# The hand-over from the delta rule to the branch products: loads by token block, a last group kept on chip, the conv cache as side work, and the order of split products

## The chip, the cores and the metric

The kernel runs on one core of a Trainium2 chip. The metric is the time of one execution in microseconds on the device. The engines are PE (TensorE, matrix products, with a queue of weight loads PEld), DVE (VectorE), ACT (ScalarE), POOL (GpSimd) and SP (SyncE, which here only issues DMAs).

## The reference

One layer of a hybrid decoder for 1024 prompt tokens and 8 x 4 sample tokens, in float32:

```python
z = _rmsnorm(x, g_attn) @ w_in           # split into q, k, v, gates, ...
qkv, new_conv = _causal_conv(concat([qa, ka, va]), conv_buf, w_conv_a)
o_a, s_delta_new = _gated_delta(q, k, v, beta, g, s_delta)     # 4 heads, chunks of 64
o_a = _head_rmsnorm(o_a, g_out_a) * silu(oga);  y_a = o_a @ w_branch_a
o_b, s_hgrn_new = _hgrn2(qh, 1.0 - f, ib, log(f), s_hgrn)      # 4 heads, chunks of 32
o_b = _head_rmsnorm(o_b, g_out_b) * silu(ogb);  y_b = o_b @ w_branch_b
mix = sigmoid(gate_a) * y_a + sigmoid(gate_b) * y_b
x = x + mix @ w_out
x = x + (silu(conv(h2 @ w_ffn_gate)) * (h2 @ w_ffn_up)) @ w_ffn_down,  h2 = _rmsnorm(x, g_ffn)
```

Outputs are the final normed tokens, the last 3 rows ahead of the qkv convolution (`new_conv`), the states of both mixers, and the last rows of the FFN convolution. Model width is 1024, a head has 128 columns.

## The kernel before

Tokens lie along the free axis: T = 1024 + 32 = 1056 columns, in three blocks (NB) of BW = 352. A float32 operand of a large product is split in a high and a low half (`split`, L85 to L87: ACT casts the high half, L86, and DVE subtracts it for the low one, L87). A product of two split operands is three matmuls (`mm3`, L110 to L116): L114 high x high, L115 high weights x low data, L116 low weights x high data. `load_w` loads a weight tile `wraw` and splits it into `whi` and `wlo`, in pools of two buffers.

The span runs through these stages: norm and first projections (0 to 57 us), groups of the HGRN2 mixer (180 to 430), four groups of the gated delta rule (`gdn_group`, 256 tokens each, 430 to 783), the branch products (800 to 890), the product with `w_out`, and the FFN with its down product (1000 to 1760).

The projections that the groups don't need at once form a queue, `fill`. Each generator of a group yields numbers as it goes, and `drive` hands each to `fill`, which emits as many projection steps; a step is 24 matmuls 128x352. So the groups' chains of small work (DVE, ACT, DMA round trips) are woven with `fill` products on PE. Every second yield, `drive` also takes one step of the first generator in `side`. A scheduler then fixes the order of each engine.

In a `gdn_group`, L731 and L732 make `UA`; DMAs take its diagonal blocks to DRAM and back as `Db`; DVE inverts them in 15 steps (L765, L767); DMAs carry the result `X` over DRAM to `Yd`; after a `yield 2.4`, DVE transposes it (`Xd`, L780) and PE goes on at L786, L794, L807 and further small products to L869. `head_post` norms the group's output `o_sb` (L596), transposes it on PE (L603) and gates it (L605) into `og`, which L887 stores to `oT_d[0]`. `og` was loaded at L885 from `og_d`; its tile has the tag "z" of pool `mz`, two buffers.

After the four groups `store_conv_cache` transposes 12 tiles of `cout` on PE (L250), copies them on ACT (L252) to `rowt`, also tag "z", and stores that (L253, L254). Then the pool `post` opens. Three loads bring both mixers' outputs from `oT_d` into `raw` (L1184), with fill steps between; the rest of the queue drains; ACT and DVE split `raw` into `ohi` and `olo`, in blocks of 352 columns (the first block head by head, the others two heads at a time). `ohi` and `olo` take the buffers of `hhi` and `hlo`, which the fill products read. The last fill products make the gates, `sg` (L570, ACT), stored to `sg_d` (L571). The branch products follow: for each pair of output tiles and block, gates `sga` and `sgb` are loaded (L1208), four outputs are made in the four banks of `psd` (tile `pd`), DVE multiplies each with its gate (L1215), adds (L1216) and the sum is split to `mhi` and `mlo`. SP issues loads in order, and every engine's instructions run in the order of the scheduler.

## Time and profile before

| | us |
|---|---|
| median of 3 runs | 1765.17 (1764.98, 1765.17, 1772.67) |
| profiled execution | 1772.35 |
| its span | 1770.6 |
| PE busy in the span | 1723.2 |

The rows below come from the profiled execution. A timeline row is start, duration, engine, line, operation, tiles as out<-in, shape and count; brackets at its end give the idle time ahead of it and what ended it. Durations of PE are modelled and overlap: products of 128x352 that are 0.32 us long start 0.16 us apart.

### The profile page before, as it was taken

What the parts mean: (1) busy time and instruction counts of PE and PEld (TensorE: products, weight loads), DVE (VectorE), ACT (ScalarE), POOL (GpSimd) and SP (SyncE); (2) the same over time, 40 slices, a digit from 0 to 9 for tenths busy, and PEclk for the clock granted to TensorE, in tenths of its full rate; (3) what the DMA queues carried; (4) which work ended last, traced back from release to release, by engine and by line L of the source; (5) the groups of instructions that cost most, each with busy time, mean ns of one, the idle gap of its engine ahead of it and who ended that gap; (6) DMA issues with size and microseconds to landing.
All of it is one profiled execution on the core that took longest, in us unless ns stands there. A gap on an engine that the chain in (4) does not pass through costs nothing.

```text
span 1770.6 us, 31215 instructions
## 1 busy us (share of the span) xinstructions
PE 1723.2 (97%) x13345; PEld 1629.3 (92%) x13345; DVE 839.5 (47%) x1448; ACT 535.2 (30%) x1249; POOL 138.0 (8%) x226
## 2 busy tenths in 40 slices
PE   7999999999999999989999999999999999999998
PEld 7999899989989998889999999989989989899887
DVE  5411546785545444426642634443453453444446
ACT  5443324443343434123110522212212112122134
POOL 2200001120102110100000100000000000000001
PEclk9999999999999999899999999999999999999999
DMA  6333334445253532245433111120110210210203
GB/s 205 108 96 107 108 110 152 141 121 158 78 162 93 170 110 86 57 161 178 122 98 90 54 49 35 38 72 25 48 48 24 72 48 24 72 48 24 72 28 112
DMA packets 200647, 159.52 MB, mean 90 GB/s; under 512 B 18638, under 2 KB 185184, under 8 KB 200489
## 3 DMA queue, kind: packets, MB, share of 16 engines
q1 hardware_dynamic: 171286, 119.14, 22.9%
q10 hardware_dynamic: 29222, 38.39, 6.3%
q8 instruction: 105, 1.72, 0.4%
q14 instruction: 34, 0.28, 0.0%
HBM read 117.74 MB, written 39.69 MB: 89 GB/s over the span
## 4 chain that ended last, share of the span: by engine, by line
PE 84%; DVE 6%; DMA 5%; issue 2%; ACT 2%; POOL 1%; SPq 1%; ACTq 0%; DVEq 0%; POOLq 0%
PE pd L114 20%; PE pd L116 20%; PE pd L115 20%; PE pd L1342 5%; PE pd L1344 4%; PE pd L1343 4%; DMA oT_d<-og 1%; DVE co L236 1%; DVE Pt L765 1%; DVE X L767 1%; PE pm L1010 1%; PE pm L1333 1%; DMA qf<-qf_d 1%; DMA Sb<-in_state_delta 1%; PE pm L191 0%
## 5 line engine op out<-in xcount | busy, mean ns | idle before, releaser
L114 PE MATMUL pd<-hhi,whi 128*128 128x352 f32 x1056 | 351.1, 332 | 0.0
L116 PE MATMUL pd<-hhi,wlo 128*128 128x352 f32 x1056 | 347.3, 329 | 0.0
L115 PE MATMUL pd<-hlo,whi 128*128 128x352 f32 x1056 | 346.7, 328 | 0.0
L114 PE MATMUL pd<-mhi,whi 128*128 128x352 f32 x1056 | 341.3, 323 | 0.0
L115 PE MATMUL pd<-mlo,whi 128*128 128x352 f32 x1056 | 339.1, 321 | 0.0
L116 PE MATMUL pd<-mhi,wlo 128*128 128x352 f32 x1056 | 339.0, 321 | 0.0
L87 DVE TENSOR_TENSOR wlo<-wraw,whi 128x1024 fp32r<-128x1024 f32 x126 | 153.5, 1227 | 203.3 <-ACT whi L86 201.6
L86 ACT CAST whi<-wraw 128x1024 fp32r<-128x1024 f32 x126 | 130.6, 1051 | 336.6 <-PE pd L1344 135.6
L114 PEld LDWEIGHTS pd<-hhi,whi 128*128 128x128 f32 x1056 | 201.5, 191 | 2.5 <-issue 1.4
L115 PEld LDWEIGHTS pd<-hlo,whi 128*128 128x128 f32 x1056 | 201.8, 191 | 1.2 <-issue 0.2
L116 PEld LDWEIGHTS pd<-hhi,wlo 128*128 128x128 f32 x1056 | 201.5, 191 | 1.0
L115 PEld LDWEIGHTS pd<-mlo,whi 128*128 128x128 f32 x1056 | 198.9, 188 | 0.4
L114 PEld LDWEIGHTS pd<-mhi,whi 128*128 128x128 f32 x1056 | 198.7, 188 | 0.4
L116 PEld LDWEIGHTS pd<-mhi,wlo 128*128 128x128 f32 x1056 | 198.5, 188 | 0.0
L1342 PE MATMUL pd<-whi,act 128*128 128x512 f32 x352 | 138.1, 392 | 0.0
L1343 PE MATMUL pd<-wlo,act 128*128 128x512 f32 x352 | 137.2, 390 | 0.0
L1344 PE MATMUL pd<-whi,act 128*128 128x512 f32 x352 | 137.2, 390 | 0.0
L1354 DVE TENSOR_TENSOR x<-x,pd 128x512 f32<-128x512 f32 x144 | 97.8, 686 | 78.8 <-PE pd L1344 78.8
L86 ACT CAST act<-ga 128x352 fp32r<-128x352 f32 (+1 forms) x66 | 31.5, 477 | 180.6 <-DVE ga L1314 180.5
L1342 PEld LDWEIGHTS pd<-whi,act 128*128 128x128 f32 x352 | 66.1, 188 | 21.0 <-DVE ga L1314 7.5
L1314 DVE TENSOR_TENSOR ga<-pd,ga 128x352 f32<-128x352 f32 x66 | 34.5, 522 | 100.8 <-PE pd L116 100.8
L223 ACT COPY z<-pd 128x352 f32<-128x352 f32 (+1 forms) x102 | 44.2, 441 | 124.7 <-PE pd L116 124.6
(417 smaller groups left out, 2568.3 us busy)
## 6 DMA issues: line engine op xcount, KB each, us to landing
wraw<-in_w_in SPq DMA_DIRECT2D x48, 512.0 KB
wraw<-in_w_ffn_gate SPq DMA_DIRECT2D x22, 512.0 KB
wraw<-in_w_ffn_up SPq DMA_DIRECT2D x22, 512.0 KB
wraw<-in_w_ffn_down SPq DMA_DIRECT2D x22, 512.0 KB
sg_d<-sg ACTq DMA_DIRECT2D x16, 528.0 KB
qkv_d<-sl ACTq DMA_DIRECT2D x12, 512.0 KB
sga<-sg_d SPq DMA_DIRECT2D x12, 352.0 KB
sgb<-sg_d SPq DMA_DIRECT2D x12, 352.0 KB
```

The source lines that it names most:

```text
L86: nc.scalar.copy(out=hi, in_=src)
L87: (eng or nc.vector).tensor_tensor(lo, src, hi.bitcast(F32), ALU.subtract)
L114: nc.tensor.matmul(ps, whi[:, kw], xhi[:, kx], start=q == 0, stop=False)
L115: nc.tensor.matmul(ps, whi[:, kw], xlo[:, kx], start=False, stop=False)
L116: nc.tensor.matmul(ps, wlo[:, kw], xhi[:, kx], start=False, stop=q == n - 1)
L223: nc.scalar.copy(out=z[:, pad + a:pad + e], in_=ps[:, :e - a])
L236: nc.vector.scalar_tensor_tensor(co, z[:, q:q + cw], wT[:, q:q + 1], co, ALU.mult, ALU.add)
L1314: nc.vector.tensor_tensor(a[:, bs], ps, a[:, bs], ALU.mult)
L1342: nc.tensor.matmul(ps, ahi[:, s0 + k, ts], W[0][:, k, qs], start=a, stop=False)
L1343: nc.tensor.matmul(ps, ahi[:, s0 + k, ts], W[1][:, k, qs], start=False, stop=False)
L1344: nc.tensor.matmul(ps, alo[:, s0 + k, ts], W[0][:, k, qs], start=False, stop=b)
L1354: nc.vector.tensor_tensor(x1[:, t, qs], x1[:, t, qs], ps, ALU.add)
```

## The change

- In `mm3`, the second and third products change places: high x high, low weights x high data, high weights x low data.
- `ogl`, a tile of its own, takes the place of `og` in the last delta group; it isn't stored to `oT_d` (L887). The split of `raw` reads those 256 columns of the delta heads from `ogl` instead.
- `raw` is loaded by five DMAs in place of three: the first 352 columns of each mixer, then the rest; no fill steps stand between them.
- `store_conv_cache` becomes the generator `conv_cache_steps` (a `yield 0.1` after each four tiles). For the qkv cache it is appended to `side`, behind `gdn_sample`.
- `Db` takes the buffer of `ad`; `yield 2.4` becomes 2.7; `sga` leaves the tag "sl" for two buffers of its own in the pool `br`, which gets `reuse_waits="tile"`.

```diff
--- before.py
+++ after.py
@@ -112,8 +112,8 @@
         n = len(ks)
         for q, (kw, kx) in enumerate(ks):
             nc.tensor.matmul(ps, whi[:, kw], xhi[:, kx], start=q == 0, stop=False)
-            nc.tensor.matmul(ps, whi[:, kw], xlo[:, kx], start=False, stop=False)
-            nc.tensor.matmul(ps, wlo[:, kw], xhi[:, kx], start=False, stop=q == n - 1)
+            nc.tensor.matmul(ps, wlo[:, kw], xhi[:, kx], start=False, stop=False)
+            nc.tensor.matmul(ps, whi[:, kw], xlo[:, kx], start=False, stop=q == n - 1)
 
     NS = NBAT * STEP
 
@@ -204,6 +204,7 @@
     og_d = [dram.tile([H, P, SEQ], F32, name=f"og_d{x}") for x in range(2)]
     oT_d = [dram.tile([H, P, T], F32, name=f"oT_d{x}") for x in range(2)]
     sg_d = [dram.tile([KD, P, T], F32, name=f"sg_d{x}") for x in range(2)]
+    ogl = gp.tile([P, H, GW], F32, name="ogl", bufs=1)
     dU = dram.tile([NG, 2, 32, 16, 16], F32, name="dU")
     dX = dram.tile([NG, 32, 32, 16], F32, name="dX")
 
@@ -240,7 +241,11 @@
         nc.scalar.activation(dst_s.rearrange("p (b t) -> p b t", t=STEP), cs, AF.Silu)
         yield
 
-    def store_conv_cache(src, ntile, r, dst_p, dst_s, pool, tag):
+    def store_conv_cache(*args):
+        for _ in conv_cache_steps(*args):
+            pass
+
+    def conv_cache_steps(src, ntile, r, dst_p, dst_s, pool, tag):
         npad = dst_p.shape[0]
         for k0 in range(0, ntile, 4):
             k1 = min(ntile, k0 + 4)
@@ -252,6 +257,7 @@
             nc.scalar.copy(out=rowt[:, :w], in_=ps[:r, :w])
             nc.scalar.dma_start(out=dst_p[:, k0 * P:k1 * P], in_=rowt[0:npad, :w])
             nc.scalar.dma_start(out=dst_s[:, k0 * P:k1 * P], in_=rowt[npad:, :w])
+            yield 0.1
 
 
     cwT = const.tile([P, 12, 28], F32, name="cwT")
@@ -740,7 +746,7 @@
                 (nc.sync, nc.scalar)[k].dma_start(out=dU[g, k, b:32:4].rearrange("c j i -> j c i"),
                                                   in_=UA[r0:r0 + 16, :, 0, r0:r0 + 16])
 
-        Db = mp.tile([P, 16, 16], F32, name="Db", bufs=1)
+        Db = mp.tile([P, 16, 16], F32, name="Db", tag="ad", bufs=1)
         for b in range(4):
             nc.sync.dma_start(out=Db[32 * b:32 * b + 32], in_=dU[g, b // 2])
         X = mp.tile([P, 8, 16], F32, name="X", bufs=1)
@@ -775,7 +781,7 @@
                 (nc.sync, nc.scalar)[k].dma_start(out=Yd[r0:r0 + 16, :, 16 * k:16 * k + 16],
                                                   in_=dX[g, b:32:4, 16 * k:16 * k + 16].rearrange("c s r -> s c r"))
         nc.gpsimd.memset(W5[:, :, 16:32], 0.0)
-        yield 2.4
+        yield 2.7
 
         nc.vector.transpose(Xd, Yd)
         pw = PSM()
@@ -881,11 +887,12 @@
             St = Sn
             yield 1.0
         need(*[("og", 0, h) for h in range(H)])
-        og = mz.tile([P, H, GW], F32, name="og", tag="z")
+        og = ogl if g == NG - 1 else mz.tile([P, H, GW], F32, name="og", tag="z")
         nc.sync.dma_start(out=og, in_=og_d[0][:, :, gs].rearrange("h p t -> p h t"))
         yield from head_post(0, o_sb, oss, eq, og, group_cols)
-        nc.scalar.dma_start(out=oT_d[0][:, :, gs].rearrange("h p t -> p h t"), in_=og)
-        if g == NG - 1:
+        if g < NG - 1:
+            nc.scalar.dma_start(out=oT_d[0][:, :, gs].rearrange("h p t -> p h t"), in_=og)
+        else:
             nc.scalar.dma_start(out=dl_p[0, 0].rearrange("h d e -> d h e"), in_=St)
         return St
 
@@ -1163,10 +1170,10 @@
         St = drive(hgrn_group(g, St, attn, ad))
     need(*[("qkv", k, h) for k in range(3) for h in range(H)])
     side.append(gdn_sample())
+    side.append(conv_cache_steps(cout, 12, 27, cq_p[0, 0], cq_s.rearrange("l b t c -> (l b t) c"), mz, "z"))
     St = None
     for g in range(NG):
         St = drive(gdn_group(g, St))
-    store_conv_cache(cout, 12, 27, cq_p[0, 0], cq_s.rearrange("l b t c -> (l b t) c"), mz, "z")
     for gen in side:
         drive(gen)
     mixp.close()
@@ -1177,33 +1184,33 @@
     mhi = post.tile([P, KD, T], F32R, name="mhi", tag="m0")
     x1s = post.tile([32, D], F32, name="x1s")
     last = (NG - 1) * GW
-    for x, a, b in ((1, 0, T), (0, 0, last), (0, last, T)):
-        if a:
-            fill.step()
-            fill.step()
+    for x, a, b in ((0, 0, BW), (1, 0, BW), (0, BW, last), (1, BW, T), (0, SEQ, T)):
         nc.sync.dma_start(out=raw[:, x * H:(x + 1) * H, a:b], in_=oT_d[x][:, :, a:b].rearrange("h p t -> p h t"))
     fill.drain()
     nc.sync.dma_start(out=x1s, in_=x_rows(NC))
     ohi = hslot(0, [P, 2 * H, T], F32R, "ohi")
     olo = hslot(1, [P, 2 * H, T], F32R, "olo")
     for nb in range(NB):
-        bs = slice(nb * BW, (nb + 1) * BW)
         w = 2 if nb else 1
         for h in range(0, 2 * H, w):
-            split(ohi[:, h:h + w, bs], olo[:, h:h + w, bs], raw[:, h:h + w, bs])
+            a, b = nb * BW, (nb + 1) * BW
+            cols = [(a, b, raw, 0)]
+            if nb == NB - 1 and h < H:
+                cols = [(a, last, raw, 0), (last, SEQ, ogl, last), (SEQ, T, raw, 0)]
+            for a, b, o, c in cols:
+                split(ohi[:, h:h + w, a:b], olo[:, h:h + w, a:b], o[:, h:h + w, a - c:b - c])
     mlo = post.tile([P, KD, T], F32R, name="mlo", tag="m1")
     wba = I["w_branch_a"].rearrange("l k n -> (l k) n")
     wbb = I["w_branch_b"].rearrange("l k n -> (l k) n")
     rpx = ExitStack()
     rp = rpx.enter_context(tc.tile_pool(name="res", bufs=3))
-    with tc.tile_pool(name="br", bufs=1) as bp:
+    with tc.tile_pool(name="br", bufs=1, reuse_waits="tile") as bp:
         for d0 in range(0, KD, 2):
             hi, lo = load_w([[(H, wba[:, d * P:(d + 1) * P]), (H, wbb[:, d * P:(d + 1) * P])] for d in (d0, d0 + 1)])
             for nb in range(NB):
                 bs = slice(nb * BW, (nb + 1) * BW)
-                sga = gp.tile([P, T], F32, name="sga", tag="sl")
-                sgb = bp.tile([P, 2, BW], F32, name="sgb")
-                sgs = (sga[:, :2 * BW].rearrange("p (d t) -> p d t", t=BW), sgb)
+                sgs = [bp.tile([P, 2, BW], F32, name="sga", bufs=2), bp.tile([P, 2, BW], F32, name="sgb")]
+                sgb = sgs[1]
                 for x in range(2):
                     nc.sync.dma_start(out=sgs[x], in_=sg_d[x][d0:d0 + 2, :, bs].rearrange("d p t -> p d t"))
                 for x in range(2):
```

SP issues the loads of `raw` around the end of group 3. `oT_d_92` is the delta mixer's output, `oT_d_93` the HGRN2 mixer's. Before:

```order
L1208 DMA sga<-sg_d_94 128x2x352
L1184 DMA raw<-oT_d_93 128x4x1056
L1184 DMA raw<-oT_d_92 128x4x768
L1184 DMA raw<-oT_d_92 128x4x288
L1186 DMA x1s<-in_x_sample 32x1024
```

After:

```order
L1188 DMA raw<-oT_d_92 128x4x352
L1188 DMA raw<-oT_d_93 128x4x352
L1188 DMA raw<-oT_d_92 128x4x416
L1188 DMA raw<-oT_d_93 128x4x704
L1188 DMA raw<-oT_d_92 128x4x32
L1190 DMA x1s<-in_x_sample 32x1024
L1215 DMA sga<-sg_d_94 128x2x352
L1215 DMA sgb<-sg_d_95 128x2x352
```

The gate load `sga` now stands behind the loads of `raw`, with `x1s` (sample rows) between, and the delta mixer's first block comes first.

DVE from the gating of the last group to the first branch products (L1215, which is L1222 after). Before:

```order
L605 SCALAR_TENSOR_TENSOR og<-pm,ga_c,og 128x4x128 x2
L87 TENSOR_TENSOR olo<-raw,ohi 128x352 x8
L87 TENSOR_TENSOR olo<-raw,ohi 128x2x352 x8
L1215 TENSOR_TENSOR sga<-pd,sga 128x352 x2
L1215 TENSOR_TENSOR sgb<-pd,sgb 128x352 x2
L87 TENSOR_TENSOR wlo<-wraw,whi 128x8x128
```

After:

```order
L611 SCALAR_TENSOR_TENSOR ogl<-pm,ga_c,ogl 128x4x128 x2
L87 TENSOR_TENSOR olo<-ogl,ohi 128x2x256
L87 TENSOR_TENSOR olo<-raw,ohi 128x352 x8
L87 TENSOR_TENSOR olo<-raw,ohi 128x2x352 x2
L87 TENSOR_TENSOR olo<-raw,ohi 128x2x64 x2
L87 TENSOR_TENSOR olo<-ogl,ohi 128x2x256
L87 TENSOR_TENSOR wlo<-wraw,whi 128x8x128 x2
L87 TENSOR_TENSOR olo<-raw,ohi 128x2x352 x2
L87 TENSOR_TENSOR olo<-raw,ohi 128x2x32 x2
L87 TENSOR_TENSOR olo<-raw,ohi 128x2x352 x2
L1222 TENSOR_TENSOR sga<-pd,sga 128x352 x2
```

The subtraction for `olo` is in more pieces, and two of `wlo`, the weights of the next pair of output tiles, now stand among them, ahead of the first product with a gate.

PE at the transposes of the last group's output (L603, L609 after). Before:

```order
L603 MATMUL pm<-ident,o_sb 128x128 x8
L250 MATMUL pm<-ident,cout 27x128 x12
L114 MATMUL pd<-hhi,whi 128x352
L115 MATMUL pd<-hlo,whi 128x352
L116 MATMUL pd<-hhi,wlo 128x352
L114 MATMUL pd<-hhi,whi 128x352
```

After:

```order
L609 MATMUL pm<-ident,o_sb 128x128 x8
L114 MATMUL pd<-hhi,whi 128x352
L115 MATMUL pd<-hhi,wlo 128x352
L116 MATMUL pd<-hlo,whi 128x352
L114 MATMUL pd<-hhi,whi 128x352
L115 MATMUL pd<-hhi,wlo 128x352
```

The transposes of `cout` have gone from here (three times four of them stand in group 2 now), and the product with the low data half comes third.

SP in group 0, the loads of `og` and of the sample states `Sb`. Before:

```order
L627 DMA Sb<-in_state_delta 128x4x128 x2
L100 DMA wraw<-in_w_in 128x8x128 x2
L885 DMA og<-og_d_90 128x4x256
L627 DMA Sb<-in_state_delta 128x4x128
L885 DMA og<-og_d_90 128x4x256
L683 DMA x_5789<-qkv_d 128x4x256 x2
L627 DMA Sb<-in_state_delta 128x4x128
L885 DMA og<-og_d_90 128x4x256
L627 DMA Sb<-in_state_delta 128x4x128 x2
```

After:

```order
L633 DMA Sb<-in_state_delta 128x4x128 x2
L100 DMA wraw<-in_w_in 128x8x128
L891 DMA og<-og_d_90 128x4x256
L100 DMA wraw<-in_w_in 128x8x128
L891 DMA og<-og_d_90 128x4x256
L689 DMA x_5790<-qkv_d 128x4x256
L633 DMA Sb<-in_state_delta 128x4x128
L689 DMA x_5790<-qkv_d 128x4x256
L891 DMA ogl<-og_d_90 128x4x256
```

The third load of this kind goes to `ogl`; the one for group 2 stands later.

## Rows read from the trace of the kernel before

**Rows 1.** The page's busy times, one line for all engines

```profile
PE 1723.2 (97%) x13345; PEld 1629.3 (92%) x13345; DVE 839.5 (47%) x1448; ACT 535.2 (30%) x1249; POOL 138.0 (8%) x226
```

**Rows 2.** Busy time and granted clock of stretches of the span

```profile
core 0: us, PE busy (x) PEld busy (x) DVE busy (x) ACT busy (x) POOL busy (x), PEclk, DMA share, GB/s
...
739.00:756.00 17.00, 17.00 (x263) 14.32 (x264) 3.82 (x9) 3.14 (x7) 0.78 (x2) 0.50 0.01 2
...
783.00:800.00 17.00, 8.24 (x54) 7.94 (x51) 1.36 (x4) 3.73 (x9) 0.00 (x0) 0.81 0.89 321
...
795.00:804.00 9.00, 3.35 (x11) 3.15 (x12) 5.05 (x10) 7.39 (x16) 0.00 (x0) 0.50 0.69 202
...
1000.00:1600.00 600.00, 599.74 (x3448) 560.78 (x3448) 267.12 (x355) 133.84 (x283) 23.66 (x38) 1.00 0.16 46
```

**Rows 3.** Timeline of PE around the end of the last group: start, duration

```profile
769.63 1.06 PE L869 MATMUL pm<-ut,UA 128*128 128x128 f32 x8
...
790.92 0.32 PE L116 MATMUL pd<-hhi,wlo 128*128 128x352 f32 x1
...
800.65 0.95 PE L114 MATMUL pd<-ohi,whi 128*128 128x352 f32 x2 [9.41 <-ACT ohi L86]
...
810.04 0.33 PE L114 MATMUL pd<-ohi,whi 128*128 128x352 f32 x1
```

**Rows 4.** Timeline of ACT in the same stretch

```profile
783.99 0.38 ACTq L887 DMA_DIRECT2D oT_d<-og  x1
...
795.49 0.57 ACT L252 COPY rowt<-pm 27x512 f32<-27x512 f32 x1 [12.15 <-DMA oT_d<-og]
...
798.06 0.46 ACT L570 ACTIVATE sg<-pd 128x352 f32<-128x352 f32 x1 [0.68 <-DMA out<-rowt]
```

**Rows 5.** ACT's casts in 796 to 812, by shape

```profile
L86 ACT CAST ohi<-raw 128x704 fp32r<-128x704 f32 x8 | 5.5, 776 | 0.0
...
L86 ACT CAST ohi<-raw 128x352 fp32r<-128x352 f32 x8 | 3.3, 481 | 0.1
```

**Rows 6.** Timeline of DVE at the first products of the branches

```profile
798.93 10.10 DVE L87 TENSOR_TENSOR olo<-raw,ohi 128x352 fp32r<-128x352 f32 x16 [15.63 <-ACT ohi L86]
...
808.94 0.95 DVE L1215 TENSOR_TENSOR sga<-pd,sga 128x352 f32<-128x352 f32 x2
```

**Rows 7.** DVE's subtractions of the split in 796 to 890, by shape

```profile
L87 DVE TENSOR_TENSOR wlo<-wraw,whi 128x1024 fp32r<-128x1024 f32 x8 | 9.7, 1216 | 0.0
...
L87 DVE TENSOR_TENSOR olo<-raw,ohi 128x704 fp32r<-128x704 f32 x8 | 6.5, 885 | 0.0
...
L87 DVE TENSOR_TENSOR olo<-raw,ohi 128x352 fp32r<-128x352 f32 x8 | 3.7, 521 | 15.6 <-ACT ohi L86 15.6
```

**Rows 8.** Timeline of PE, starts that follow idle time, and one of group 2

```profile
526.08 0.65 PE L636 MATMUL pm<-Sb,zc 128*32 128x128 f32 x16 [1.00 <-DMA Sb<-in_state_delta]
...
562.88 0.73 PE L786 MATMUL pm<-Xd,UA 32*32 32x16 f32 x64 [1.01 <-DVE Xd L780]
...
615.45 0.33 PE L699 MATMUL pm<-ident,x 128*128 128x128 f32 x1 [1.85 <-DVE Sb L666]
...
663.34 0.73 PE L786 MATMUL pm<-Xd,UA 32*32 32x16 f32 x64 [1.35 <-DVE Xd L780]
673.92 1.16 PE L851 MATMUL pm<-St,x 128*128 128x128 f32 x8
...
692.25 0.66 PE L603 MATMUL pm<-ident,o_sb 128*128 128x128 f32 x4 [1.77 <-DVE o_sb L596]
...
738.96 0.99 PE L786 MATMUL pm<-Xd,UA 32*32 32x16 f32 x64 [2.50 <-DVE Xd L780]
```

**Rows 9.** Timeline of SP, DMA issues in group 0

```profile
521.28 0.36 SPq L885 DMA_DIRECT2D og<-og_d  x1
```

**Rows 10.** Timeline of DVE in group 3, ahead of the chain of L765

```profile
720.33 1.22 DVE L87 TENSOR_TENSOR wlo<-wraw,whi 128x1024 fp32r<-128x1024 f32 x1
```

**Rows 11.** Timeline of PE at the first products of the program

```profile
13.25 0.59 PE L115 MATMUL pd<-ibw,hhi 128*128 128x264 f32 x1 [0.20 <-DVE ibw L87]
```


## The prediction

> **What bounds the kernel now.** I read the busy times first: PE is busy for 1723.2 of 1770.6 us, so all that can be won without taking work away is about 47 us of idle time and what PE loses at the lower of its two clock levels [rows 1, 2]. The stretches come next: in 1000 to 1600 PE is busy for 599.74 of 600 us, so nothing outside PE's own work counts there [rows 2]. Then the timeline of PE for each start that follows idle time. The largest gap is 9.41 us, ahead of the first branch product at 800.65 [rows 3]; gaps of 1.0 to 2.5 us lie in the four delta groups [rows 8]. Last I read what stands behind the large gap. ACT's second `rowt` copy waited 12.15 us for the store `oT_d<-og`, because `rowt` and `og` share two buffers, and the last `sg`, a third copy and all `ohi` casts stand behind it on ACT, so PE starts 2.6 us after the sg of 798.06 [rows 3, 4]. All this is one execution of 1772.35 us, 7.2 us above the median of 1765.17. Work and order are the same in both, so I take the surplus for clock loss of that execution; I subtract only idle time and losses that belong to the order, and subtract them from the median.
>
> **The transition, the main term.** Call T the end of the last fill product, 791.1 before (790.92 plus one spacing of 0.16) [rows 3]. Before, the fifth output of the branch products starts at 810.04, T + 18.9. The 48 products of the first four outputs took 9.39 us from 800.65; about 12 of them ran at half clock, 11 in 3.35 us, 0.30 each, which leaves (9.39 - 3.6) / 36 = 0.16 for the others [rows 2, 3].
>
> After, `oT_d` of the last group is neither stored nor loaded, and no `rowt` stands on ACT. Five loads, 2048 bytes x 1856 columns = 3.80 MB, wait for the L869 products of the last chunk, which end at about 770.7 [rows 3]. At 321 GB/s, as in 783 to 800 [rows 2], they take 11.8 us and land at about 783 to 785. They land before T because T itself stays: the same PE work lies ahead of it. If this cover of 6 us is gone, each us late is a us of gap. Behind T stand one cast from `ogl` (512 columns, between 0.48 and 0.78, I take 0.6, begun 0.2 before T), the last sg (0.46) and one cast (0.48) [rows 4, 5]: PE restarts at about T + 1.4, and 48 products at 0.16 end at T + 9.1.
>
> PE then needs a free bank: PSD has four, and the fifth output waits for the first product of line L1222 (L1215 before) on DVE. Before, DVE had that done by about 809.5, just ahead of PE [rows 6]. The order of DVE after puts all of `olo` and, new, two `wlo` subtractions ahead of it. The `olo` instructions sum to 8 x 0.521 + 8 x 0.885 = 11.25 us of durations and take 10.10 in a row, a factor of 0.90 [rows 6, 7]. After there are 8 of 352, 6 of 704, one of 512 left (0.69), 2 of 128 and 2 of 64 columns (0.29 and 0.22 by the line through the two measured shapes): 11.2 x 0.9 = 10.1, with two wlo at 1.216 x 0.9 = 2.2 and the eviction at 0.5. DVE is there at T + 1.4 + 12.8 = T + 14.2. So a new stall of 14.2 - 9.1 = 5.1 us stands where the old gap was, in front of the fifth output, and the fifth output moves from T + 18.9 to T + 14.2: 4.7 won, not 9. ACT is no bound there: its casts are shorter than DVE's [rows 5, 7].
>
> The clock goes back after such a stall: it was 0.50 in 795 to 804, around the 9.41 us gap, and again in 739 to 756 behind 2.50 us [rows 2, 8]. Twelve products at 0.30 in place of 0.16 cost 1.7; I take 1.5. The bounds are 0 (no fall) and 8.5 (half of a stretch as long as 739 to 756). The transition gives 4.7 - 1.5 = **3.2**. The Trainium skill (TensorE: Matmul & The Clock Gate, HAM oscillation) says that waits between bursts of matmuls put the clock back and that each fall is paid again; by it the 1.5 is due, without it the transition would be 4.7.
>
> **The delta groups.** `conv_cache_steps` moves 12 transposes, 3 copies and 6 stores into group 2, and no fill step is kept back for the loads, so the planner spreads fill products differently. I counted them in the order between the last L731 and L786. Group 1: 151 before, 165 after, 14 x 0.16 = 2.2 us more cover over a gap of 1.01: **1.0**. Group 2: 162 and 164: **0.3** of 1.35. Group 3: 159 and 154, 0.8 us less cover; but of the two wlo around L760 of which one (1.22) holds L765 back, both come ahead of it after, about 1.4 us earlier: net **0.6** of 2.50, between -0.8 and 1.4 [rows 8, 10]. At 615.45, 13 more products stand ahead of the chain to L666: up to 1.85. At 692.25, 9 more stand ahead of L603: up to 1.4 of 1.77. At 526.08 the gap of 1.00 waits for an `Sb` load which SP issued behind the `og` load of 521.28, one that had waited for a store; after, the third such load goes to `ogl` and waits for nothing [rows 8, 9]. These three rest on what stands in a queue and not on a chain that I could follow to its end, so I take half: **0.9, 0.7 and 0.5**, between 0 and full.
>
> What the moved steps cost: on ACT three copies of 0.57 and six store issues stand in group 2 ahead of L801 and L859 [rows 4]. The transposes are the same work at another place, and lie under the fill products. `Db` takes the dead buffer of `ad`: no wait for a living tile, nothing. `sga` with two buffers of its own: its loads no longer wait for the last `sl`, nothing on the path. The raw loads move ahead of sga on SP, which is needed only at T + 14.
>
> **The order of the triple.** High x low comes last, so that `olo` may be late by one product. At the start of the program the second product waits 0.20 for the low half of `ibw`; after, it waits for that of `hlo`, made behind it: **-0.2**, between -0.6 and 0.2 [rows 11]. Two products with the same weights stood side by side before and stand apart after. PE's weight loads number 13345, as many as its products, so every product had its own load before as well: nothing is lost [rows 1]. The Trainium skill (TensorE: Matmul & The Clock Gate, Step-by-step) says that weights typically stay for many products, loaded once; by that rule a third of the loads would be new after, but this trace shows a load for each product already, and the sum by the trace has zero.
>
> **Sum.** 3.2 + 1.0 + 0.3 + 0.6 + 0.9 + 0.7 + 0.5 - 0.2 = 7.0 us. 1765.2 - 7.0 = **1758.2**; against the profiled execution the same step gives 1765.4.
>
> **Rivals.** (A) All count-based gains come in full and the stall doesn't bring the clock down: 4.7 + 1.0 + 0.3 + 0.6 + 1.85 + 1.4 + 1.0 - 0.2 = 10.65, **1754.5**. For it: each gap is shorter than the cover added. Against it: the half clock on both sides of gaps of this size [rows 2, 8]. (B) Given back: only the transition, group 1 and group 2 come, and group 3 keeps its wlo wait and loses 0.8: 3.2 + 1.0 + 0.3 - 0.8 = 3.7, **1761.5**. For it: the chain in group 3 is the longest gap of the groups, with 17 us at half clock behind it [rows 2, 8]. (C) Slower: the third `rowt` copy of group 2 takes the first one's buffer and stands on ACT ahead of L859, which PE waits for. The first store leaves at about 665.5, the third copy is due when L851 starts at 673.92, 8.4 us later [rows 8]. Each us that the store takes beyond 8.4 is a us of PE. A store of 12.15, as the wait of rows 4, costs 3.7, 1762; above the median plus 8.8 it gets once a store takes 8.4 + 7.0 + 8.8 = 24 us, **1774**. Against it: these stores are a tenth of `oT_d<-og` and have no 321 GB/s of loads beside them. (D) It doesn't do what it says: the loads land so late that the gap stays 9.4; DVE's queue then ends at T + 22, 3.3 later than before, and with 3.8 from the groups it is **1764.7**.
>
> **Chances.** Forecast 0.33, A 0.32, B 0.22, C 0.07, D 0.06. About 0.5% (8.8 us) is what a measurement of this kernel can tell from no change: below 1756.3 lie most of A and some of the forecast's own spread, 0.39; above 1774.0 lies C with the far end of the clock bound, 0.09; between them 0.52. The range runs from 1751 (A, with some clock loss gone that the median still has) to 1767 (B and D with a longer half-clock stretch).
>
> **What would show it.** Transition: PE idle about 1.4 us ahead of the first product with `ohi`, then about 5 us ahead of the fifth output, released by DVE on L1222; all raw loads landed before T. A clock of 0.50 right behind that stall. Groups: no idle time ahead of L786 in group 1, less than 2.5 in group 3. ACT in group 2: no `rowt` copy with a wait above 1 us. The forecast is wrong if the fifth output starts with no stall, if PE idles in group 2 for ACT, or if the triples of 128x352 space themselves differently from 0.16.

## The result, and the profile of the changed kernel

The changed kernel takes 1749.21 us in the median (1747.41 to 1750.57, 4 runs). The ratio to the kernel before is 0.9887, with a 95% interval of 0.9864 to 0.9911. The forecast of 1758.2 was too high by 9.0 us and the result lies just below the range. The kernel before, run beside every experiment below, has a median of 1769.5 us over 57 runs (1761.9 to 1782.1); the 1765.17 of the three first runs lies in its lower part.

The profiled execution of the changed kernel takes 1749.61 us, with a span of 1747.9, against 1772.35 and 1770.6: 22.7 us less. Its page has for the engines:

```profile
PE 1709.4 (98%) x13345; PEld 1617.7 (93%) x13345; DVE 844.3 (48%) x1452; ACT 537.0 (31%) x1253; POOL 133.6 (8%) x226
```

Against [rows 1], the idle time of PE falls from 47.4 to 38.5 us, 8.9 less, and its busy time by 13.8, though it executes the same 13345 products. The second part is the larger one in this pair of profiles, and it is mostly clock. The waits of PE, summed by what ended them (total, number, longest):

```profile
engine line waited for: us in total, times, longest us
...
PE pd L114 <- DVE sga L1222: 4.7, 1, 4.7
...
PE pm L792 <- DVE Xd L786: 1.5, 2, 1.2
...
PE pd L114 <- ACT ohi L86: 1.3, 1, 1.3
```

The 9.4 us for `ohi` has become 1.3, and a wait of 4.7 us for DVE's L1222 is new. The waits ahead of the small products of a delta group, 5.2 us in four before (group 0 has 0.34; the others are in [rows 8]), are 1.5 in two. The stretches of both kernels by granted clock, after first (columns as in [rows 2]: stretch, length, busy time of PE, PEld, DVE, ACT, POOL with counts, clock, DMA share, GB/s):

```profile
core 0: us, PE busy (x) PEld busy (x) DVE busy (x) ACT busy (x) POOL busy (x), PEclk, DMA share, GB/s
...
434.00:438.00 4.00, 4.00 (x17) 4.00 (x16) 0.69 (x1) 3.13 (x3) 0.00 (x0) 0.57 1.05 272
...
729.00:746.00 17.00, 16.98 (x315) 14.90 (x315) 7.99 (x16) 6.15 (x13) 0.78 (x2) 1.00 0.30 96
...
785.00:789.00 4.00, 3.46 (x12) 3.49 (x13) 3.08 (x6) 0.78 (x1) 0.00 (x0) 0.58 0.56 167
...
976.00:980.00 4.00, 4.00 (x18) 4.00 (x17) 3.92 (x7) 4.00 (x10) 0.71 (x2) 0.60 0.44 127
...
990.00:1580.00 590.00, 590.00 (x3388) 551.47 (x3386) 262.30 (x342) 128.60 (x267) 16.09 (x36) 1.00 0.15 45
```

and three short ones of before, beside the long one of [rows 2]:

```profile
363.00:367.00 4.00, 4.00 (x69) 3.66 (x56) 3.41 (x6) 2.58 (x9) 1.69 (x2) 0.58 0.59 201
...
565.00:569.00 4.00, 4.00 (x22) 3.78 (x24) 0.74 (x2) 1.80 (x5) 0.78 (x2) 0.57 0.02 4
...
616.00:620.00 4.00, 4.00 (x20) 4.00 (x19) 1.89 (x6) 3.87 (x13) 1.04 (x1) 0.57 0.50 146
```

A clock of 0.57 over 4 us means some 3.4 us at 1.2 GHz. Summed over the span while PE had work, the kernel before ran 37.4 us at this level: 3.4 each around 363, 435, 565, 616 and 998, 17.1 from 739.1, and 3.3 behind the gap at 800. The changed kernel ran 10.2: around 434, 785 and 976. If half of the time at half clock is lost, that makes (37.4 - 10.2) / 2 = 13.6 us. This is an estimate, and rather a high one, since the small products lose less: 64 of them took 0.99 us at half clock in [rows 8] and take 0.73 at full clock below. The busy time of PE fell by 13.8, so idle time and clock account for nearly all of the difference: 8.9 + 13.6 = 22.5 of 22.7. Behind the small products of group 3 PE was fully busy in both kernels, before with 263 products in 17 us at 0.50 [rows 2], after with 315 in 17 us at full clock (729 to 746). The FFN gave nothing: PE is busy for 590.00 of 590 us, as it was in [rows 2].

One pair of profiles overstates the clock's part. The span and the mean granted clock are on record for 53 runs of the kernel before and for nine of the changed one (the four above and five in the experiments). The product (1 - clock) x span, an estimate of what half clock cost, is 20.3 us in the mean before (10.6 to 32.0) and 7.6 after. Some 3.5 of the 20.3 fall into the gap of 9.41 us, where PE has nothing to run (the clock is 0.81 over 783 to 800 in [rows 2]). So by this estimate some 9 of the 18.1 us between the mean times are clock, and about as much is waits.

The transition, on PE (start, duration; brackets: idle time and what ended it):

```profile
772.97 0.43 PE L114 MATMUL pd<-ohi,whi 128*128 128x352 f32 x1 [1.29 <-ACT ohi L86]
...
785.54 0.53 PE L114 MATMUL pd<-ohi,whi 128*128 128x352 f32 x1 [4.66 <-DVE sga L1222]
```

and on DVE:

```profile
772.21 0.69 DVE L87 TENSOR_TENSOR olo<-ogl,ohi 128x512 fp32r<-128x512 f32 x1 [3.38 <-ACT ohi L86]
...
772.95 5.66 DVE L87 TENSOR_TENSOR olo<-raw,ohi 128x352 fp32r<-128x352 f32 x12
...
778.53 0.69 DVE L87 TENSOR_TENSOR olo<-ogl,ohi 128x512 fp32r<-128x512 f32 x1
...
779.13 2.36 DVE L87 TENSOR_TENSOR wlo<-wraw,whi 128x1024 fp32r<-128x1024 f32 x2
...
781.40 3.56 DVE L87 TENSOR_TENSOR olo<-raw,ohi 128x704 fp32r<-128x704 f32 x6
...
784.88 0.95 DVE L1222 TENSOR_TENSOR sga<-pd,sga 128x352 f32<-128x352 f32 x2
```

T, the end of the last fill product, is 772.97 - 1.29 = 771.7. The fifth output starts at 785.54, T + 13.9, and the 48 products ahead of it end 4.66 us earlier. DVE's row of 2.36 us for two `wlo` stands in the middle of its `olo` rows, and its first L1222 starts as the last `olo` ends.

The small products of groups 1 to 3:

```profile
562.01 0.73 PE L792 MATMUL pm<-Xd,UA 32*32 32x16 f32 x64
...
655.24 0.73 PE L792 MATMUL pm<-Xd,UA 32*32 32x16 f32 x64 [1.16 <-DVE Xd L786]
...
729.70 0.73 PE L792 MATMUL pm<-Xd,UA 32*32 32x16 f32 x64
```

Groups 1 and 3 have no idle time there any more, where [rows 8] has 1.01 and 2.50. In group 3, the store of `sg`, the transfers of the inverse and DVE's transpose stand at:

```profile
721.05 0.34 ACTq L577 DMA_DIRECT2D sg_d<-sg  x1
...
722.39 1.74 SPq L777 DMA_DIRECT2D dX<-X  x4
...
724.92 1.74 SPq L781 DMA_DIRECT2D Yd<-dX  x4
...
728.48 0.45 DVE L786 STREAM_TRANSPOSE Xd<-Yd 128x256 f32<-128x256 f32 x1 [6.15 <-DMA Yd<-dX]
```

DVE has transposed the result at 728.93, 6.5 us after the first dX issue. The same leg took 8.7 before, where ACT had issued a store of `sg` just ahead of the dX transfers:

```profile
730.00 0.34 ACTq L571 DMA_DIRECT2D sg_d<-sg  x1
...
730.23 2.13 SPq L771 DMA_DIRECT2D dX<-X  x4
...
738.46 0.45 DVE L780 STREAM_TRANSPOSE Xd<-Yd 128x256 f32<-128x256 f32 x1 [8.29 <-DMA Yd<-dX]
```

Now that store leaves at 721.05. No run moves the store alone, but over the 14 profiles the leg of group 3 goes with it: 8.5 and 8.7 us where the store left 0.2 us ahead of the first dX, 7.4 and 7.9 at 0.9 us, 6.5 to 7.2 at 1.3 us or more in nine profiles. One profile is an exception (no side work: 7.9 at 1.6 us).

### The profile page after: what moved, and what is told of

It is laid out like the page before. It is cut to its first block, busy times and chain, and to the rows that moved or that the text cites. A ratio compares the mean times of both kernels' runs of the same rounds, so it can differ in the third digit from the quotient of the medians.

```text
span 1747.9 us, 31213 instructions
## 1 busy us (share of the span) xinstructions
PE 1709.4 (98%) x13345; PEld 1617.7 (93%) x13345; DVE 844.3 (48%) x1452; ACT 537.0 (31%) x1253; POOL 133.6 (8%) x226
## 4 chain that ended last, share of the span: by engine, by line
PE 86%; DVE 6%; DMA 3%; issue 2%; ACT 2%; POOL 1%; SPq 0%; ACTq 0%; POOLq 0%; DVEq 0%
PE pd L114 21%; PE pd L115 21%; PE pd L116 21%; PE pd L1349 5%; PE pd L1351 4%; PE pd L1350 4%; DVE co L237 1%; PE pm L1340 1%; PE pm L1017 1%; DMA oT_d<-og 1%; DVE olo L87 1%; PE pm L737 1%; DVE Pt L771 0%; DVE wlo L87 0%; PE pm L873 0%
## 5 line engine op out<-in xcount | busy, mean ns | idle before, releaser
L116 PE MATMUL pd<-hlo,whi 128*128 128x352 f32 x1056 | 343.2, 325 | 0.0
L235 DVE TENSOR_SCALAR co<-z,fwT 128x1072 f32<-128x1072 f32 x22 | 17.1, 778 | 176.1 <-ACT z L226 176.1
```

The source lines that it names most:

```text
L116: nc.tensor.matmul(ps, whi[:, kw], xlo[:, kx], start=False, stop=q == n - 1)
```

## The experiments

Theory 1 after the result: the missing part of the sum is half clock, which follows waits in the delta groups, so what shortens those waits counts for more than its idle time. The rival: the transition is worth more than the forecast said. The runs take single parts of the change. Each kernel ran beside the kernel before.

**The yield alone** (the kernel before with this):

```diff
-        yield 2.4
+        yield 2.7
```

> The kernel before with one number changed: yield 2.7 in place of 2.4 ahead of L780. Theory 1 (the half-clock stretches of the delta groups are the missing gain, and they go with the wait at L786 of group 3): the fill products are spread so that group 1 has 17 more ahead of L786, both wlo of group 3 come ahead of L760, and the sg store leaves one fill output earlier, away from the dX and Yd transfers. The chain of group 3 is then some 3 us shorter against 10 products (1.6 us) less cover, so the wait of 2.50 falls below 1 us and the 17 us at half clock behind it go. Expected: 1756 to 1760 us against 1769 of before, no stretch at half clock in group 3. Rival (the gain comes from the transition and from idle time alone): 1766 to 1769, since group 1 gives 1.0 and group 3 loses 1.6 of cover.

Measured: 1769.25 us, ratio 1.0017 (0.9995 to 1.0039). The expectation fell. The products of PE and the stretch behind them in group 3:

```profile
736.43 0.73 PE L786 MATMUL pm<-Xd,UA 32*32 32x16 f32 x64 [1.86 <-DVE Xd L780]
...
737.00:744.00 7.00, 7.00 (x130) 6.21 (x119) 1.88 (x5) 1.61 (x4) 0.78 (x2) 0.55 0.01 2
```

The wait there is 1.86, not below 1: the chain from the first dU issue to the transposed `Xd` is 24.1 us long against 25.6 before, 1.5 shorter and not 3, and 10 products of cover (1.6 us) are lost. The half clock behind it was 6.8 us in this execution, the fastest of the ten; the runs spread from 1763.8 to 1778.0, and their mean (1 - clock) x span is 20.7 us, as in the kernel before. By itself the yield moves cover from groups 2 and 3 to group 1 and gains nothing.

**The transition alone** (the kernel before with `ogl`, the five loads, `sga` in `br`, and `Db` in the buffer of `ad` for room):

```diff
+    ogl = gp.tile([P, H, GW], F32, name="ogl", bufs=1)
-    for x, a, b in ((1, 0, T), (0, 0, last), (0, last, T)):
-        if a:
-            fill.step()
-            fill.step()
+    for x, a, b in ((0, 0, BW), (1, 0, BW), (0, BW, last), (1, BW, T), (0, SEQ, T)):
...
```

> The kernel before with ogl, the five loads of raw and the two buffers for sga (and Db in ad's buffer, which makes the room); product order, yield and conv cache as before. Theory 1: the groups are as before, with the wait of 2.5 us and 17 us at half clock in group 3; only the transition changes, and since the conv cache stands at the end of the groups as before, ACT still has three rowt copies there, but none waits for oT_d. Fifth output about 4 to 5 us earlier: 1763 to 1766 us. Rival (the transition is the main gain): 1755 or less.

Measured: 1759.85 us, ratio 0.9958 (0.9941 to 0.9975). Between the two theories: 7 to 9 us, more than the 3.2 of the forecast and less than half of the whole, and below the 1763 to 1766 of theory 1.

```profile
735.54 0.73 PE L787 MATMUL pm<-Xd,UA 32*32 32x16 f32 x64 [2.30 <-DVE Xd L781]
...
738.00:742.00 4.00, 4.00 (x46) 3.30 (x46) 1.27 (x3) 1.95 (x5) 0.78 (x2) 0.59 0.01 4
...
783.80 0.59 PE L114 MATMUL pd<-ohi,whi 128*128 128x352 f32 x2 [1.71 <-ACT ohi L86]
...
795.02 0.40 PE L114 MATMUL pd<-ohi,whi 128*128 128x352 f32 x1 [1.11 <-DVE sga L1217]
...
783.04 1.22 DVE L87 TENSOR_TENSOR wlo<-wraw,whi 128x1024 fp32r<-128x1024 f32 x1 [8.89 <-ACT whi L86]
...
783.80:793.90 10.10, 9.73 (x48) 9.16 (x48) 10.10 (x21) 9.58 (x20) 0.00 (x0) 0.83 0.75 237
```

The wait of group 3 stays (2.30), with half clock behind it for 3.4 us only, and the mean (1 - clock) x span of the ten runs is 11.6 us against 20.3. Theory 1 doesn't explain this: by it the loss should have stayed with the wait. The fifth output comes at T + 12.9 (T = 782.1), 6.0 earlier than before and 0.9 earlier than in the full change: one `wlo` of 1.22 us stands ahead of the first product with a gate, where the full change has two. The wait for DVE is only 1.1 us because PE comes later too: it restarts at T + 1.7, waits another 0.37 for `olo`, which stands behind that `wlo`, and runs the 48 products at a mean clock of 0.83. With `ogl`, the gaps at 526 and 615 [rows 8] are also down, to 0.39 and 0.54, while the one at 563 grew from 1.01 to 1.71.

**The product order alone** (the kernel before with the two lines of `mm3` exchanged):

```diff
-            nc.tensor.matmul(ps, whi[:, kw], xlo[:, kx], start=False, stop=False)
-            nc.tensor.matmul(ps, wlo[:, kw], xhi[:, kx], start=False, stop=q == n - 1)
+            nc.tensor.matmul(ps, wlo[:, kw], xhi[:, kx], start=False, stop=False)
+            nc.tensor.matmul(ps, whi[:, kw], xlo[:, kx], start=False, stop=q == n - 1)
```

> The kernel before with the product order of mm3 of the change alone. Theory 1: 6 products more ahead of L786 in group 1 and 4 more in group 3; one wlo of group 3 leaves from ahead of L765; the sg store stays beside the dX transfer. The wait of group 3 falls from 2.5 to about 1 us. If a stretch at half clock needs a wait of that size it may stay: 1761 to 1767 us. Rival (the order itself costs, since equal weights stand apart): slower than 1769, with products of 128x352 further apart than 0.16 us.

Measured: 1763.49 us, ratio 0.9968 (0.9949 to 0.9987), in the range of theory 1; the order isn't free, it gains about 6 us.

```profile
731.51 0.98 PE L786 MATMUL pm<-Xd,UA 32*32 32x16 f32 x64 [1.82 <-DVE Xd L780]
...
731.00:752.00 21.00, 20.49 (x280) 17.69 (x281) 6.93 (x15) 4.06 (x7) 0.78 (x2) 0.52 0.14 49
```

The wait in group 1 is gone, the one in group 3 is 1.82 and not the expected 1, and the half clock behind it lasted 20.5 us.

**The yield undone** (the changed kernel with `yield 2.4`).

> The changed kernel with yield 2.4 in place of 2.7. Theory 1 (what is missing in the sum is half clock behind the wait ahead of the small products of group 3): the fill products ahead of them go from 154 to 163 and one wlo of group 3 moves, as in the run of the product order alone, which had a wait of 1.82 us there and 20 us at half clock; wait and stretch come back here. Expected: 1753 to 1759 us, with runs several us apart as before the change. Rival (the group's wait is not what separates the kernels, transition and side work are): 1748 to 1751, runs within 3 us as with the change.

Measured: 1751.69 us (1749.48 to 1753.44), ratio 0.9897 (0.9849 to 0.9945). A wait of 1.23 us came back in group 3, but in this profile no half clock behind it, only 3.4 us behind the 0.87 us wait of group 2. The median lies between the two that the changed kernel has (1749.21 and 1752.76), so no effect of the yield shows in the changed kernel; the expected 1753 to 1759 didn't come.

**The order undone** (the changed kernel with the second and third products exchanged back).

> The changed kernel with the product order of before. The spread of fill products is that of the run with the yield alone (149 ahead of the small products of group 3, 153 in group 2), which had waits of 1.86 and 0.97 there. Theory 1: a wait of about 1.5 to 2 us in group 3, half clock behind it, 1753 to 1759 us and a wide spread. Rival (the order counts for nothing, as the sum had it): 1748 to 1751.

Measured: 1758.10 us (1755.61 to 1767.68), ratio 0.9939 (0.9911 to 0.9965), in the range of theory 1: 5 to 9 us lost by one exchange of lines, against the two medians of the changed kernel. But it didn't come as theory 1 said, by a wait of 1.5 to 2 us in group 3:

```profile
563.84 0.73 PE L792 MATMUL pm<-Xd,UA 32*32 32x16 f32 x64 [0.91 <-DVE Xd L786]
...
566.00:580.00 14.00, 14.00 (x138) 11.67 (x133) 4.81 (x10) 2.07 (x5) 1.25 (x4) 0.51 0.35 99
```

Waits stand ahead of the small products of all four groups again (0.51, 0.91, 0.97 and 0.86), and 13.7 us at half clock follow that of group 1.

**The order in one half of the program** (the changed kernel; order[0] is -1 for the order of before):

```diff
+            mid = ((wlo, xhi), (whi, xlo))[::order[0]]
-            nc.tensor.matmul(ps, wlo[:, kw], xhi[:, kx], start=False, stop=False)
-            nc.tensor.matmul(ps, whi[:, kw], xlo[:, kx], start=False, stop=q == n - 1)
+            nc.tensor.matmul(ps, mid[0][0][:, kw], mid[0][1][:, kx], start=False, stop=False)
+            nc.tensor.matmul(ps, mid[1][0][:, kw], mid[1][1][:, kx], start=False, stop=q == n - 1)
```

> The changed kernel with the product order of before in everything up to the last fill product, and the order of the change from the branch products on. If the order acts by where the fill products fall in the delta groups, this is the run with the order undone: 1755 to 1760 us, with waits of some 7 us in the groups. Rival (the order acts in the branch products, the product with w_out or the FFN): 1748 to 1751.

> The mirror image: the order of the change up to the last fill product, the order of before from the branch products on. If the order acts by the fill products alone: 1748 to 1751 us, and about 0.3 us more wait for olo at the first branch product. Rival: 1755 to 1760.

Measured: with the order of before up to the last fill product 1758.44 us, ratio 0.9936 (0.9912 to 0.9960); with the order of before from the branch products on 1751.55, ratio 0.9892 (0.9875 to 0.9909). The changed kernel, run again beside them, expected and measured:

> The changed kernel once more, for the comparison with the other runs of this call: 1747 to 1751 us, since its delta groups have no long wait ahead of the small products.

1752.76 us (1749.19 to 1758.17, 5 runs), ratio 0.9900 (0.9879 to 0.9922), 3.6 us above its first four runs. So the order acts ahead of the branch products alone. It is hardly by the products' own time: in the FFN, products of 128x352 have mean durations of 321 to 323 ns before and after the change. And here it isn't clock: with the order of before in the fill, the mean (1 - clock) x span is 8.8 us, as in the repeat of the changed kernel (8.8), while PE idles for 14.8 us from 425 us to T and not for 6.4 (2.2 of the 14.8 are a pause of PE that the profile puts down to no wait). What differs is where the scheduler lets the fill products fall. Counted in the order, 633 of them stand between the last L731 and the small products of the four groups with the new order (150, 165, 164, 154), 620 with the old one (150, 168, 153, 149). These 13 products are 2.1 us at 0.16 each, less than the idle time that comes with them, so how the rest follows isn't shown.

**No side work** (the changed kernel with `store_conv_cache` after the groups).

> The changed kernel with the conv cache stored after the groups, as before, in place of side work. In its order of DVE no wlo stands ahead of the first L1222. If the stall of 4.7 us is DVE's queue, 2.2 us of wlo less leave about 2.5 us of it, while three rowt copies of 0.57 and their stores stand ahead of the first casts again, so PE waits 1.3 + 1.1 or more for the first ohi. Sum: 1748 to 1751 us, no change, with a shorter stall at the fifth output and a longer one at the first. Rival (the side work in group 2 is what made the delta groups shorter): 1753 or more.

Measured: 1750.13 us, ratio 0.9896 (0.9871 to 0.9920), no change, as expected. The four counts of fill products are the same as with side work. On PE and DVE:

```profile
773.29 0.43 PE L114 MATMUL pd<-ohi,whi 128*128 128x352 f32 x1 [0.41 <-ACT ohi L86]
...
784.87 0.63 PE L114 MATMUL pd<-ohi,whi 128*128 128x352 f32 x1 [3.49 <-DVE sga L1222]
...
784.20 0.95 DVE L1222 TENSOR_TENSOR sga<-pd,sga 128x352 f32<-128x352 f32 x2
...
785.92 1.22 DVE L87 TENSOR_TENSOR wlo<-wraw,whi 128x1024 fp32r<-128x1024 f32 x1
```

No `wlo` stands ahead of L1222 here, the first `wlo` row comes behind it, and the wait for DVE is 3.49. Expected were 2.5: PE resumed after 0.41 us and not later, because one `ohi` cast now stands ahead of the last `sg`. That gives the 0.9 us that it has to wait more at the fifth output. The fifth output comes at T + 12.0 against T + 13.9: 1.9 us earlier, for two `wlo` of 2.36 us that are out of the way. What this wins is lost ahead of it: up to T, PE idles for 9.8 us, against 7.5 and 6.4 in the two profiles of the changed kernel.

**olo on POOL** (three kernels; the first is the changed one with this):

```diff
-                split(ohi[:, h:h + w, a:b], olo[:, h:h + w, a:b], o[:, h:h + w, a - c:b - c])
+                split(ohi[:, h:h + w, a:b], olo[:, h:h + w, a:b], o[:, h:h + w, a - c:b - c],
+                      nc.gpsimd if nb == 2 or (nb == 1 and h >= H) else None)
```

> The changed kernel with the olo subtractions of the third block, and of the second block of the HGRN2 heads, on POOL in place of DVE. If the stall of 4.7 us ahead of the fifth output is DVE's queue (10.1 us of olo, 2.2 of wlo), DVE is at its first L1222 after 8 x 0.521 and 2 x 0.885 times 0.9, 2.2 of wlo and 0.5, some 8 us behind the first cast, against 7.7 us of products: the stall falls below 1 us, and with it the 3.4 us at half clock behind it. Expected 1742 to 1745 us. Rival (POOL is too slow or slows DVE down): the stall moves to a later olo, 1748 to 1752.

Measured: 1746.89 us, ratio 0.9889 (0.9861 to 0.9917).

```profile
774.64 5.62 DVE L87 TENSOR_TENSOR olo<-raw,ohi 128x352 fp32r<-128x352 f32 x10 [4.08 <-ACT ohi L86]
...
780.71 3.61 DVE L87 TENSOR_TENSOR wlo<-wraw,whi 128x1024 fp32r<-128x1024 f32 x2 [0.45 <-ACT whi L86]
...
784.24 0.94 DVE L1223 TENSOR_TENSOR sga<-pd,sga 128x352 f32<-128x352 f32 x2
...
784.89 0.40 PE L114 MATMUL pd<-ohi,whi 128*128 128x352 f32 x1 [1.96 <-DVE sga L1223]
```

Expected were 1742 to 1745, by the rival 1748 to 1752. The wait for DVE falls from 4.66 to 1.96, not below 1: two `wlo` on DVE take 3.61 us beside POOL's work, 2.36 without it.

With the whole second and third block on POOL (`nc.gpsimd if nb else None`):

> As the run with olo on POOL, with the whole second and third block on POOL. DVE is at its first L1222 after 8 x 0.521 times 0.9, 2.2 of wlo and 0.5, 6.5 us behind the first cast, ahead of PE's 7.7: no stall for L1222. POOL has two pieces of 704 columns to do before the fifth output, which takes it some 4 us. Expected 1743 to 1746 us. If POOL is late with them, PE waits for olo and the time stays at 1747.

Measured: 1750.14 us, ratio 0.9897 (0.9845 to 0.9949); the wait stays at 1.94, and one of 0.47 follows; the expected 1743 to 1746 didn't come.

With the first split and the two `wlo` on POOL as well:

> The run with olo partly on POOL, with the two wlo subtractions of the second weight pair on POOL as well. DVE then has 8 x 0.521 and 2 x 0.885 times 0.9 and 0.5 ahead of PE's fifth output, 5.9 us behind the first cast, against 7.7 us of products: the 2.0 us that were left of the stall go. Expected against the repeat of the changed kernel: 4 to 6 us less, 1743 to 1746. Rival: POOL's olo for the HGRN2 heads of the second block come late behind its two wlo (about 1.9 us each), and PE waits for those instead.

Measured: 1748.69 us, ratio 0.9878 (0.9860 to 0.9896). The wait for L1222 is gone, and the rival came true:

```profile
788.06 0.43 PE L116 MATMUL pd<-olo,whi 128*128 128x352 f32 x1 [2.26 <-POOL olo L87]
...
780.96 5.42 POOL L87 TENSOR_TENSOR wlo<-wraw,whi 128x1024 fp32r<-128x1024 f32 x2
...
786.34 7.16 POOL L87 TENSOR_TENSOR olo<-raw,ohi 128x704 fp32r<-128x704 f32 x6
```

PE waits 2.26 us for POOL's `olo`, which stands behind 5.42 us of `wlo` there. Against the repeat of the changed kernel beside it this is 4 us less, the low end of the expected 4 to 6, but the intervals overlap: no version that surely beats the change was found.

**Waits and clock together.** For each profile, the idle time of PE from 425 us to T (the brackets of its timeline, summed) and the time at half clock in the same stretch. For all runs, the mean of (1 - clock) x span, which counts half clock over the whole span (2 to 3.5 us of it in the long gap of the first three kernels, where PE idles), with the number of runs, and the median:

| kernel | idle, us | half clock, us | (1 - clock) x span, us (runs) | median, us |
|---|---|---|---|---|
| before | 12.8 | 27.3 | 20.3 (53) | 1769.5 |
| yield alone | 13.9 | 6.8 | 20.7 (10) | 1769.3 |
| order alone | 12.4 | 20.5 | 16.7 (10) | 1763.5 |
| transition alone | 11.8 | 6.8 | 11.6 (10) | 1759.9 |
| changed, old order in the fill | 14.8 | 13.7 | 8.8 (6) | 1758.4 |
| changed, old order | 11.1 | 17.1 | 12.7 (10) | 1758.1 |
| changed, yield 2.4 | 9.4 | 3.4 | 9.2 (4) | 1751.7 |
| changed, order of before at the end | 7.1 | 3.4 | 8.3 (4) | 1751.6 |
| changed, no side work | 9.8 | 3.4 | 7.6 (9) | 1750.1 |
| changed, POOL (three kernels) | 9.8, 8.1, 7.5 | 0, 6.8, 3.4 | 4.4, 9.6, 6.1 (4 each) | 1746.9, 1750.1, 1748.7 |
| changed (two profiles) | 7.5, 6.4 | 3.4, 3.4 | 6.1 (4), 8.8 (5) | 1749.2, 1752.8 |

The half clock of one profile is one draw, and the column of all runs is the surer one: the yield alone drew 6.8 and loses as much as the kernel before over its runs. In that column, kernels with less than 10 us of waits lose 4 to 10 us, and those with more lose 11 to 21, with one exception: the old order in the fill has the longest waits and loses 8.8.

## Why the prediction was wrong, point by point

**The base and the clock: the step that failed.** "I subtract only idle time and losses that belong to the order, and subtract them from the median." This set clock loss aside as a chance surplus of the profiled execution (7.2 us), and gave no term to the rest. But the loss stands in nearly every run: the mean clock of 53 runs of the kernel before is 0.982 to 0.994, with a median of 0.988, against 0.986 in the profile. So a term is missing from the sum. Of its 7.0 us, some 6.7 are idle time (9.4 - 1.4 - 5.1 = 2.9 in the transition, 4.0 in the groups, -0.2 at the start); measured are 8.9, which is near. For the clock the sum has 0.2, the 1.7 us of the 12 slow products of before less the 1.5 behind the new stall; measured are 13.6 in the two profiles, and some 9 in the mean of the runs. The base itself was 4.4 us low, the median of three runs against that of 57. That error brought the forecast nearer to the result, by luck: from 1769.5 the same sum gives 1762.5.

**Clock.** Of the 13.6 us, 8.5 are the 17.1 us behind the wait in group 3. I used that stretch as a bound for a loss (8.5 us, in the transition), and not as something that the change could take away. Its wait was forecast to shrink from 2.50 to 1.9; it went to zero. That the stretch went because the wait did is not shown: in the run of the transition alone the wait is 2.30 and the stretch 3.4 us. The chain from `UA` to the transposed `Xd` became 3.1 us shorter (706.5 to 728.9, before 713.3 to 738.9). Some 1.0 of it lies ahead of the first dX issue, where I had 1.4 for `wlo`; 2.1 lie in the round trips dX and Yd, which no longer run beside the store of `sg` and which the forecast left as they were.

**The order of the triple.** Forecast -0.2, measured a gain of 6 (alone) and of 5 to 9 us (undone). The cost was right (at the start of the program the fourth product begins 1.97 us behind the first, 1.77 before); what the order does to the work of the scheduler was left out. I counted the fill products ahead of the small ones correctly and put the difference down to side work and yield. The side work moves none of them, the yield moves 17 to group 1 and takes 19 from groups 2 and 3, and the order adds 10 (to the kernel before) or 13.

**The delta groups.** Forecast 4.0 us of idle time less from 500 to T, with three terms halved; measured 6.0, from 9.7 to 3.7. Halving was wrong: the gaps at 526, 615 and 692 went, or were replaced by shorter ones (0.57 and 0.76 ahead of L670, 0.63 twice ahead of L737). Group 2 went from 1.35 to 1.16, 0.2 less, forecast 0.3.

**The transition.** Right in each step. PE restarts at T + 1.3 (forecast 1.4), DVE's first L1222 ends at about T + 13.7 (14.2), the new wait is 4.66 (5.1), the fifth output comes at T + 13.9 (14.2), and half clock follows, 3.4 us of it, 1.7 lost (1.5). Net 5.0 - 1.7 = 3.3, forecast 3.2. Two `wlo` ahead of L1222 are part of that stall: with none of them there (no side work) the fifth output comes 1.9 us earlier, with one (the transition alone) 0.9.

**Rivals.** A was the nearest, 1754.5, and its terms for the groups came nearly in full (6.15 us, measured 6.0); it lacked the clock. C did not come: the third `rowt` copy waits for PE, not for a store, and ACT's work for L859 behind it isn't late. The sign that the prediction named, no `rowt` copy with a wait above 1 us, was missed all the same, here (5.27 us) and at 656.55 (2.98 us), both times in a wait for PE, so it couldn't tell C from the forecast.

```profile
666.06 0.57 ACT L257 COPY rowt<-pm 27x512 f32<-27x512 f32 x1 [5.27 <-PE pm L255]
...
667.85 1.14 ACT L865 ACTIVATE t<-pm,eG 128x128 f32<-128x128 f32 x4 [1.21 <-PE pm L859]
```

D did not come: the loads were issued from 756.3 to 760.3, and PE waited for the cast, not for a load.

## What to carry to other kernels

Where PE is busy for 97% of the span, look at the granted clock of the stretches as well as at the gaps: stretches of up to 20.5 us at half clock, some 10 us of loss, stood behind waits of 1 to 2.5 us ahead of small products, so a sum for a change that touches such waits needs a term for the clock. Take that term from the clock of many runs, not from one profile, and the base of the sum too, when runs spread more than the forecast. Changing the order of instructions also changes what a scheduler puts beside them; compare the counts under each wait part by part before saying which edit moves them.

## What the runs showed of the hardware

Half clock followed waits of 0.9 to 2.5 us, with PE busy all through the stretch, and its length varied from one execution to the next behind nearly the same wait: 3.4 us behind 2.30, 6.8 behind 1.86, 20.5 behind 1.82, 13.7 behind 0.91, none behind 1.23, and none behind the waits of 1.35 and 1.77 in [rows 8] (1.00 from 620 to 739). The Trainium skill (TensorE: Matmul & The Clock Gate, HAM oscillation) tells of waits between bursts of matmuls that put the clock back. The traces agree for the wait of 4.66 us (0.58 in 785 to 789), and show the same behind shorter ones, though not each time. What decides the length stays open; none of the runs separates it. That the waits bring it is shown only by the table, as a tendency over kernels with one exception. Why the scheduler sets more fill products ahead with the new order was not tried either.

DVE and POOL slow each other when both do such subtractions: two `wlo` of 1024 columns took DVE 3.61 us instead of 2.36, and POOL's `olo` of 512 columns beside them took 2.28 where it took 1.28 before. POOL itself took 5.42 us for two `wlo` (third kernel), over twice DVE's time. POOL's rows in the first kernel:

```profile
773.94 1.28 POOL L87 TENSOR_TENSOR olo<-ogl,ohi 128x512 fp32r<-128x512 f32 x1 [11.49 <-ACT ohi L86]
...
780.95 2.28 POOL L87 TENSOR_TENSOR olo<-ogl,ohi 128x512 fp32r<-128x512 f32 x1
```
